# A two-level Winograd matmul: three more sums of A stored by the first column chunk, and a scheduler with uneven bandwidth shares

## Chip, cores and metric

One Trainium2 chip, one core of it. The metric is device time in microseconds (us): the median of several runs, here 1467.81 us before the change (three runs, 1466.79 to 1472.12).

## What is computed

`out = tanh(a @ b + bias)`, with `a` and `b` of 4096 x 4096 float32, `bias` of 4096 float32 added to each row, `out` float32. The kernel multiplies in fp16 with float32 sums in PSUM.

```python
def reference(a, b, bias):
    return np.tanh(np.matmul(a, b) + bias)
```

## The kernel before

**Tiling.** The output's 4096 columns are worked in four **chunks** of 1024 (`NCW`); the 4096 rows in 16 **pairs** of 2 x 128 rows, and two pairs (512 rows) make a **group**, in the code a `duo`, numbered 0 to 7. For one pair and one chunk the matmul is a 2 x 2 block matmul: A in four blocks a11, a12, a21, a22 of 128 rows x 2048, B in b11 to b22 of 2048 x 512. It is done with Strassen's seven products in Winograd's form (`work`, L885): P1 = a11 b11, P2 = a12 b21, P3 = s4 b22, P4 = a22 t4, P5 = s1 t1, P6 = s2 t2, P7 = s3 t3. The sums of A are s1 = a21 + a22, s2 = s1 - a11, s3 = a11 - a21 = a22 - s2, s4 = a12 - s2. A **plain** product is 16 matmuls of 128 x 128 by 128 x 512 per pair. A **fine** product does the same once more, with the two pairs of a group as the two block rows: seven smaller products (p1 to p7) of eight matmuls with 256 columns, 56 matmuls for the group in the place of 32 of double width. For a fine product the left operand is needed in three combinations of the two pairs, y, z and v (`fine_left`, L611), the right one as f1, f2, f3, f4 (`fine_right`, L749).

**Chunks.** The first chunk begins with eight 128-row blocks done as an ordinary matmul, while B arrives; then groups 2 to 7 run with Strassen at one level, and `STEEP[0]` gives how many of P1, P7, P5 are fine in each of the six groups: 0, 1, 1, 1, 1, 1. `natural` (L514) loads the four raw blocks of a pair through POOL's queue (`load_rows`, the cast to fp16 is in the DMA), transposes them on DVE, and makes the sums. The second to fourth chunk each go twice over the eight groups: `pass_one` (P1 and P2 of each group, and P6 in the last two chunks) in the order `ORDER[c]`, then `pass_two` (P7, P6, P5, P4, P3) in the reverse order.

**What is kept in HBM.** `scratch` (L409) has for each name and group a tensor with five slots of half a block: slots 1 and 2 hold the first pair p, 3 and 4 the second pair q with its halves swapped; slot 0 holds q.lo + q.hi - p.lo (`sigma`, L600). With slot 0 filled, a pass can fetch the group as a `Skew` (L569): y from slots 0 and 1, x from slots 2 and 3, without a sum on DVE. `keep` (L542) writes slots 1 to 4, `move` (L530) issues one DMA on SP's queue, 512 KB for two slots and 256 KB for one. In the first chunk groups 2 to 7 store a11, a12, a22 and s2 so. In the second chunk's second pass `lowers` (L1160) sends these groups to `all_skewed` (L1176): fetch a22, s2, a11, a12 as skews (s2 with half a block more, for its plain P6), make s3, s1 and s4 by `skew_sum`, two DVE operations of 128 x 2048 each, and store the three for the later chunks. Groups 0 and 1 aren't stored by the first chunk but for pair 0: the second chunk loads their raw blocks through POOL (`upper`, L1216, in the first pass; `others`, L1226, in the second, where the sums are made too).

**What sets the order.** Nothing is ordered by hand below that. Every operation is added to a `Plan` (L134) with an engine, an estimated duration, what it reads and writes, and for transfers the bytes. `rank` gives each a due time from its successors; `schedule` (L216) then lets five queues (PE, DVE, ACT, POOL, SP) run against each other in an event loop, takes buffers from 51 places of SBUF (`PLACES`) when an operation may start, and the order in which operations start there is the order in which they are emitted. PE keeps the order in which its work was added. On the chip each engine goes through its list in that fixed order and waits by semaphores: an operation that waits holds back all behind it. Transfers in the model share bandwidth: each has a rate and a latency (`DMA`), and `flow` (L275) gives every queue that has something under way the same share. `FARTHER` (L38) limits how far ahead of PE, in us of due time, a chunk's later loads of B (b12, b22) may be taken up.

Of the kernel before, what the change touches and what calls it, by code (L numbers as in the profile page):

```python
# [10 lines left out]
P = 128  # L11
# [6 lines left out]
TP = T // 2  # L18
# [5 lines left out]
ADD = mybir.AluOpType.add  # L24
SUB = mybir.AluOpType.subtract
# [5 lines left out]
KEPT = (("a11",), ("s1", "a22", "s4"), ("a11", "a12", "s3", "s2", "s1", "a22", "s4"), ())  # L31
NEAR = 12.0
REACH = 20.0
ORDER = ((2, 3, 4, 5, 6, 7), (7, 6, 0, 5, 1, 4, 3, 2), (2, 0, 1, 3, 4, 5, 6, 7), (7, 6, 5, 4, 3, 2, 1, 0))
SUMS = tuple(range(16))
SOFT = 1.5
BEHIND = 2
FARTHER = (50, 60, 50, 50)  # L38
THREE = (False, False, True, True)
LATER = 6  # L40
HOLD = (1, 1, 1, 1)
FIRST = (0,)
WHOLE = ()
SPARE = ("a11", "a12", "a22")
HELD = ("s1", "s3", "s4")
PLAIN = (0, 0, 0, 0)
SMALL = 5
RING = 8
DMA = {"POOL": (380e3, 3.75), "LATER": (380e3, 6.0), "in": (405e3, 3.1), "out": (315e3, 2.8)}
RISE = ((), (4, 4, 4, 4, 4, 4, 4, 4), (4, 4, 4, 4, 4, 4, 4, 4), (4, 4, 4, 4, 4, 4, 4, 4))  # L50
SECONDS = (0, 8, 8, 8)
STEEP = ((0, 1, 1, 1, 1, 1), (0, 1, 2, 2, 2, 2, 2, 2), (0, 3, 3, 3, 3, 3, 3, 3))
BASIS = ("a11", "a12", "a22", "s2")
STORED = BASIS + ("s1", "s3", "s4")
LEFT = ("P6", "P7", "P5", "P4", "P3")
# [78 lines left out]
class Plan:  # L134
# [81 lines left out]
    def schedule(self):  # L216
# [38 lines left out]
        def fits(op):  # L255
# [16 lines left out]
                    return False  # L272
            return not want or op.due <= at_pe[0] + min(op.reach, op.far if op.early else 1e9)

        def flow(now):  # L275

            live = [p for p in pipes.values() if p]
            for p in live:
                p[0][0] -= (now - clock[0]) / len(live)
            clock[0] = now  # L280
            ended = False
            for p in live:
                while p and p[0][0] < 1e-6:
                    op = p.pop(0)[1]
                    op.done = now + op.wait
                    heapq.heappush(events, (op.done, op.n, 1))
                    ended = True
            return ended

        def next_flow(now):  # L290
            live = [p for p in pipes.values() if p]
            if live:
                clock[1] += 1
                at = now + max(min(p[0][0] for p in live), 1e-6) * len(live)
                heapq.heappush(events, (at, clock[1], 3))

        while events:
# [74 lines left out]
def kernel(  # L372
# [62 lines left out]
    def tt(o, x, y, op, n, reads, writes, wide=True, **kw):  # L435
        dve(n, lambda: nc.vector.tensor_tensor(out=o(), in0=x(), in1=y(), op=op), reads, writes, wide, **kw)  # L436
# [4 lines left out]
    def at(buf, *key):  # L441
        key = key if len(key) > 1 else key[0] if key else slice(None)
        return lambda: buf[key]
# [86 lines left out]
    def move(name, duo, first, tl, t0, n, out, **kw):  # L530

        box = scratch[name, duo]
        dram_, key = (box, range(first, first + n)), (ALL, ds(t0 * TP, n * TP))
        sb = tl if out else (tl, range(t0, t0 + n))

        def emit():
            far, near = box[ALL, ds(first, n)], tl[key].rearrange("p (n t) m -> p n t m", n=n)
            nc.sync.dma_start(out=far if out else near, in_=near if out else far)

        add("SP", 0.34, emit, (sb if out else dram_,), (dram_ if out else sb,), nbytes=P * n * TP * P * 2, **kw)  # L540
# [56 lines left out]
            tt(at(o), at(u), at(v), op, T * P, (u, v), (o,), wide=False)  # L597
        return Skew(name, None, here)

    def sigma(name, duo, pq):  # L600

        p, q = (s[name] for s in pq)
        v = new("v" + name, [P, TP, P], cls="out")
        tt(at(v), at(q, ALL, ds(0, TP)), at(q, ALL, ds(TP, TP)), ADD, TP * P, (q,), (v,), wide=False, soft=6.0)
        tt(at(v), at(v), at(p, ALL, ds(0, TP)), SUB, TP * P, (v, (p, (0,))), (v,), wide=False, soft=6.0)
        move(name, duo, 0, v, 0, 1, True, soft=6.0)
        skewed.add((name, duo))

    skewed, held_names = set(), {}
# [275 lines left out]
    def work(duo, name, s, part=None, last=True):  # L885

        d, c, k, bop, pair = duo, duo.c, duo.k, duo.bop, duo.pairs[s]
        left, right, bank = {
            "P1": ("a11", "b11", D), "P2": ("a12", "b21", D), "P7": ("s3", "t3", I), "P6": ("s2", "t2", Z),
            "P5": ("s1", "t1", C), "P3": ("s4", "b22", C), "P4": ("a22", "t4", Z),  # L890
        }[name]
        bank = bank[s]
        a_ = d.a[s]
        if name == "P3" and "s4" not in a_:
            asum(a_, "s4", "a12", "s2", SUB, over=None if d.stays else "s2")
            if c == 1 and not d.parts and pair in SUMS:
                keep(pair, a_, ("s4",))
                whole.add(pair)
        t0, nt = (0, T) if part is None or name == "P3" else (part * TP, TP)
        start = name == "P1" or (name == "P7" and part != 1)  # L900
        product(bank, a_[left], [bop.get((right, i)) for i in range(4)], t0, nt, start)
        b1 = k["b1"]
        if name == "P1":
            after_p1(d, s, part)
        elif name == "P7":
            if part != 0:
                d.p7[s] = new("p7", [P, NB], fp32, "out")
                copy(at(d.p7[s]), at(bank), NB, (bank,), (d.p7[s],))
                after_p7(d, s, part)
        elif name == "P6":  # L910
            after_p6(d, s, part)
        elif name == "P5":
            if part == 0:
                return
            after_p5(d, s)
        elif name == "P2":
            if part == 0:
                e = d.aside[s] = [new("aside", [P, NB], fp32, "out" if i == 2 else "big") for i in range(0)]
                d.as11[s] = (d.box[s], 0)
                copy(at(d.box[s], ALL, 0), at(bank), NB, (bank,), ((d.box[s], (0,)),))  # L920
# [735 lines left out]
    for c in range(NC):  # L1656
        duos = [[2 * i, 2 * i + 1] for i in ORDER[c]]
        if c >= TWO:
            k = load_bias(c)
            finish_bias(k)  # L1660
            bop, rights = {}, {}
            for name in ("b11", "b21"):
                for blk in range(4):
                    raw_b(bop, c, name, blk, NEAR)
            rights["P1"] = fine_right(bop, "b11", True, NEAR)
            if SECONDS[c]:
                rights["P2"] = fine_right(bop, "b21", True, NEAR)
            if before:
                waiting.append(lambda between, before=before: (before(), between()))

            def rest():
                for blk in range(4):
                    for name in ("b12", "b22"):
                        raw_b(bop, c, name, blk, (NEAR, FARTHER[c]))
                    bsums(bop, blk, (NEAR, FARTHER[c]))

            if THREE[c]:
                rest()
                rights["P6"] = fine_right(bop, "t2", True, NEAR)
            on_chip = pass_one(c, k, bop, rights, duos, held)  # L1680
            if not THREE[c]:
                rest()
            pass_two(c, k, bop, rights, duos[::-1], on_chip)
            before = held = None
            continue
        fines = {}
        for i, pairs in enumerate(duos):
            d = Duo()
            d.c, d.k, d.bop, d.pairs = c, k, bop, sorted(pairs)
            d.parts = c > 0 and i == 0  # L1690
            d.last = d.stays = i == len(duos) - 1 and c < TWO - 1
            d.x = STEEP[c][i]
            duo = d.pairs[0] // 2
            d.a = [natural(p, p in early, i == 0, SPARE if p % 2 and duo not in WHOLE else ()) for p in d.pairs]
            for name in () if duo in WHOLE else BASIS if i == 0 else BASIS[1:]:
                sigma(name, duo, d.a)
            if d.x and not d.parts:
                for name, r in (("P1", "b11"), ("P7", "t3"), ("P5", "t1"))[:d.x]:
                    if name not in fines:
                        fines[name] = fine_right(bop, r)  # L1700
            d.right = fines
            before = run_duo(d, before)
            held = d.a
    def place_tile(buf):
# [44 lines left out]
```

## Time and profile before

| what | value |
|---|---|
| median of three runs | 1467.81 us |
| lowest, highest | 1466.79, 1472.12 us |
| the profiled execution's own time | 1469.58 us |
| its span, first to last instruction | 1467.9 us |
| DMA, mean over the span | 266 GB/s, 390.43 MB |
| POOL's queue (q0), the casting loads | 73.44 MB as written |
| SP's queue (q1) | 315.15 MB |
| second chunk's first pass, about | 405 to 520 us |
| second chunk's second pass, about | 520 to 770 us |

The profile has one execution with each instruction's start and end. PE is the tensor engine's matmuls, PEld its weight loads, DVE the vector engine, ACT the scalar engine, POOL and SP two engines that here issue transfers; a name with q (SPq, POOLq) is an engine's DMA issue. `b<-in_b_dram` reads: tile b, written from tensor in_b_dram. In names of tiles the numbers are left out, `parts` are small float32 or half-size buffers that share a place, `nat` are raw tiles of A. L436 and L439 are the helpers for all DVE sums and ACT copies, L771 and L786 the matmuls of plain and fine products; so the tiles tell them apart, not the line. In a group's line the time after the bar is its busy total, then the mean of one in ns, then the idle time of its engine just before it and what ended that.

### The profile page before, as it was taken

How to read it: one execution, taken by the hardware profiler on the slowest of the kernel's cores; microseconds unless marked ns; L12 is line 12 of the kernel's file. 1: busy time of each engine (PE TensorE's matmuls, PEld its weight loads, DVE VectorE, ACT ScalarE, POOL GpSimd, SP SyncE). 2: the span in 40 equal slices, each digit the busy share in tenths (PEclk: the TensorE clock that was granted, in tenths of full speed). 3: DMA queues.
4: the chain of work that ended last, by engine and by line, in shares of the span. 5: the costliest groups of instructions: out<-in, count | busy, mean ns of one | idle time of the engine just before them, and what ended most of it. 6: DMA issues, size and time to landing. Idle time of an engine off the chain costs nothing.

```text
span 1467.9 us, 28825 instructions
## 1 busy us (share of the span) xinstructions
PE 1445.8 (98%) x11232; PEld 1098.5 (75%) x11232; DVE 1116.6 (76%) x1716; ACT 459.6 (31%) x1056; POOL 303.7 (21%) x565
## 2 busy tenths in 40 slices
PE   9999999999999999899999999999999999999998
PEld 4444545555478877678878888888888888888887
DVE  3557877666857898888788799976778678986765
ACT  2111211121133424243343332334333333243433
POOL 8754433434333001010131300000111310000000
PEclk9999999999999999999999999999999999999999
DMA  9999999999999979999999988778999988678773
GB/s 177 190 234 259 270 244 227 262 237 228 264 273 298 333 238 327 286 345 334 336 314 322 294 267 290 234 259 272 255 286 339 244 238 292 231 246 271 262 256 110
DMA packets 196873, 390.43 MB, mean 266 GB/s; under 512 B 25728, under 2 KB 91776, under 8 KB 196736
## 3 DMA queue, kind: packets, MB, share of 16 engines
q1 hardware_dynamic: 114048, 315.15, 61.5%
q0 software_dynamic: 82688, 73.44, 32.1%
q8 instruction: 88, 1.44, 0.4%
q14 instruction: 49, 0.40, 0.1%
HBM read 320.86 MB, written 141.03 MB: 315 GB/s over the span
## 4 chain that ended last, share of the span: by engine, by line
PE 73%; DMA 16%; DVE 5%; POOL 3%; issue 2%; ACT 1%; DVEq 0%; POOLq 0%; ACTq 0%; SPq 0%
PE ps L786 54%; PE ps L771 18%; DMA b<-in_b_dram 8%; DMA nat<-in_a_dram 5%; DMA land<-in_a_dram 2%; POOL b L698 2%; POOL land L492 1%; DVE parts L436 1%; DMA st<-state 1%; DVE ps L436 0%; DMA out_dram<-parts 0%; DMA xs<-s 0%; DVE a L468 0%; DMA a<-a 0%; DVE b L436 0%
## 5 line engine op out<-in xcount | busy, mean ns | idle before, releaser
L698 POOL DMA_DIRECT2D b<-in_b_dram x256 | 137.6, 541 | 538.1 <-DVE ps L436 203.6
L439 ACT COPY ps<-ps 128x256 f32<-128x256 f32 (+1 forms) x289 | 106.0, 367 | 336.6 <-PE ps L786 322.4
L492 POOL DMA_DIRECT2D nat<-in_a_dram x240 | 129.1, 543 | 334.1 <-PE ps L786 165.9
L786 PEld LDWEIGHTS <-ya 128*128 128x128 f16 x1424 | 139.3, 98 | 17.4
L786 PEld LDWEIGHTS <-zs 128*128 128x128 f16 x1408 | 138.0, 98 | 19.0 <-DVE b L436 0.8
L786 PEld LDWEIGHTS <-xa 128*128 128x128 f16 x1152 | 112.9, 98 | 26.0 <-issue 11.4
L786 PEld LDWEIGHTS <-za 128*128 128x128 f16 x1232 | 120.6, 98 | 14.2 <-issue 0.2
L786 PEld LDWEIGHTS <-ys 128*128 128x128 f16 x1216 | 118.9, 98 | 16.1 <-DVE ys L436 2.3
L439 ACT COPY parts<-ps 128x256 f32<-128x256 f32 (+1 forms) x182 | 70.9, 390 | 163.4 <-DVE ps L436 74.8
L786 PEld LDWEIGHTS <-parts 128*128 128x128 f16 x1104 | 108.0, 98 | 12.7 <-DVE parts L436 0.3
L771 PEld LDWEIGHTS <-s 128*128 128x128 f16 x624 | 61.0, 98 | 74.7 <-DVE s L436 2.8
L436 DVE TENSOR_TENSOR parts<-ps,parts 128x256 f32<-128x256 f32 (+1 forms) x172 | 75.2, 437 | 52.8 <-PE ps L786 46.2
L771 PEld LDWEIGHTS <-a 128*128 128x128 f16 x624 | 61.0, 98 | 72.0 <-DVE a L436 1.0
L786 PEld LDWEIGHTS <-xs 128*128 128x128 f16 x1056 | 103.2, 98 | 15.0 <-issue 1.6
L1547 PE MATMUL ps<-b,o 128*128 128x512 f16 x512 | 111.4, 379 | 0.7 <-DVE ps L1572 0.6
L468 DVE STREAM_TRANSPOSE a<-nat 128x512 uint32<-128x512 uint32 x120 | 78.2, 688 | 38.3 <-PE ps L771 21.4
L436 DVE TENSOR_TENSOR ps<-ps,parts 128x256 f32<-128x256 f32 (+1 forms) x187 | 83.0, 445 | 28.6 <-PE ps L786 15.7
L786 PE MATMUL ps<-b,zs 128*128 128x256 f16 x768 | 100.2, 274 | 0.5 <-DVE b L436 0.5
L1547 PEld LDWEIGHTS <-o 128*128 128x128 f16 x512 | 49.8, 98 | 60.9 <-issue 1.2
L624 DVE TENSOR_TENSOR zs<-xs,ys 128x2048 f16<-128x2048 f16 x66 | 80.4, 1218 | 17.6 <-PE ps L786 16.1
L771 PE MATMUL ps<-t,s 128*128 128x512 f16 x400 | 88.0, 379 | 2.3 <-DVE s L436 2.3
L771 PE MATMUL ps<-b,a 128*128 128x512 f16 x384 | 85.0, 379 | 0.5 <-DVE a L436 0.5
(140 smaller groups left out, 2576.2 us busy)
## 6 DMA issues: line engine op xcount, KB each, us to landing
ya<-a SPq DMA_DIRECT2D x72, 512.0 KB, 6.3
xa<-a SPq DMA_DIRECT2D x72, 512.0 KB, 6.3
ys<-s SPq DMA_DIRECT2D x66, 512.0 KB, 5.1
xs<-s SPq DMA_DIRECT2D x66, 512.0 KB, 4.9
b<-in_b_dram POOLq DMA_DIRECT2D x256, 128.0 KB, 8.0
nat<-in_a_dram POOLq DMA_DIRECT2D x240, 128.0 KB, 7.0
out_dram<-parts SPq DMA_DIRECT2D x112, 256.0 KB, 6.2
a<-a SPq DMA_DIRECT2D x32, 512.0 KB, 6.3
```

Of the source, the lines that this page charges most:

```text
L436: dve(n, lambda: nc.vector.tensor_tensor(out=o(), in0=x(), in1=y(), op=op), reads, writes, wide, **kw)
L439: act(n, lambda: nc.scalar.copy(o(), x()), reads, writes, **kw)
L468: nc.vector.transpose(dst[ALL].rearrange("P t m -> P (t m)").bitcast(pair32).rearrange("P (U m) -> P U m", m=P)[:, ds(t0 // 2, nu), ds(row ...
L492: nc.gpsimd.dma_start(out=tl[(ds(q * QP, QP), *key)], in_=src)
L624: nc.vector.tensor_tensor(out=halves(z), in0=halves(x), in1=halves(y)[:, ds(0, 1)].broadcast_to([P, 2, TP * P]), op=SUB,)
L698: nc.gpsimd.dma_start(out=dst.rearrange("p t j n -> p t (j n)") if j is None else dst, in_=src)
L771: nc.tensor.matmul(bank[ALL], left_tile(left, k + t + shift), rb.tile(t), start=start and k == t0 and t == 0, stop=k + t == t0 + nt - 1, s ...
L786: nc.tensor.matmul(bank[ALL, HALF[half]], left_tile(buf, at_ * TP + i * TB + t), rb.tile(t), start=False, stop=i == 1 and t == TB - 1, ski ...
L1547: nc.tensor.matmul(bank[ALL], left_tile(left, t), rb.tile(tb), start=start, stop=stop, skip_group_check=True,)
```

## The change

Four things are changed. (1) Groups 2, 3, 4 and 5 also store s1, s3 and s4 in the first chunk, each with slot 0 (`AHEAD`, `put_by`), and are marked `whole`, so that the second chunk's second pass fetches s3, s2, s1, a22 and s4 and doesn't call `all_skewed` for them. Groups 6 and 7 stay as they were. (2) The second chunk's order has group 0 in fourth and group 1 in sixth place, where they were third and fifth; `STEEP[0]` ends with 2, so group 7's P7 is fine in the first chunk; `FARTHER` is 40 for the last two chunks. (3) The scheduler's rates and latencies are others, and `rates` replaces equal shares: when POOL's queue and SP's both have something under way, SP's has 0.64 if its first transfer is a load and 0.47 if it is a store, and POOL's has the rest. (4) `sigma` takes how soft its due time is.

```diff
-ORDER = ((2, 3, 4, 5, 6, 7), (7, 6, 0, 5, 1, 4, 3, 2), (2, 0, 1, 3, 4, 5, 6, 7), (7, 6, 5, 4, 3, 2, 1, 0))
+ORDER = ((2, 3, 4, 5, 6, 7), (7, 6, 5, 0, 4, 1, 3, 2), (2, 0, 1, 3, 4, 5, 6, 7), (7, 6, 5, 4, 3, 2, 1, 0))
-FARTHER = (50, 60, 50, 50)
+FARTHER = (50, 60, 40, 40)
+AHEAD = (("s1", "s3", "s4"), ("s1", "s3", "s4"), ("s1", "s3", "s4"), ("s1", "s3", "s4"), (), ())
-DMA = {"POOL": (380e3, 3.75), "LATER": (380e3, 6.0), "in": (405e3, 3.1), "out": (315e3, 2.8)}
+DMA = {"POOL": (384e3, 3.65), "LATER": (384e3, 5.0), "in": (399e3, 3.86), "out": (369e3, 3.5)}
+SHARE = (0.64, 0.47)
-STEEP = ((0, 1, 1, 1, 1, 1), (0, 1, 2, 2, 2, 2, 2, 2), (0, 3, 3, 3, 3, 3, 3, 3))
+STEEP = ((0, 1, 1, 1, 1, 2), (), ())
...
+        def rates():
+
+            live = [(e, p) for e, p in pipes.items() if p]
+            if len(live) == 1:
+                return [(live[0][1], 1.0)]
+            part = {p[0][1].eng: SHARE[p[0][1].soft is not None or not p[0][1].bufs] for _, p in live if p[0][1].hw}
+            return [(p, 1 - sum(part.values()) if e == "POOL" else part[e]) for e, p in live]
+
         def flow(now):
-
-            live = [p for p in pipes.values() if p]
-            for p in live:
-                p[0][0] -= (now - clock[0]) / len(live)
+            shares = rates() if any(pipes.values()) else []
+            for p, r in shares:
+                p[0][0] -= (now - clock[0]) * r
...
+    def put_by(d, name, s):
+
+        keep(d.pairs[s], d.a[s], (name,), spare=(name,) if s else ())
+
-    def sigma(name, duo, pq):
+    def sigma(name, duo, pq, soft=6.0):
...
         if name == "P3" and "s4" not in a_:
             asum(a_, "s4", "a12", "s2", SUB, over=None if d.stays else "s2")
-            if c == 1 and not d.parts and pair in SUMS:
-                keep(pair, a_, ("s4",))
-                whole.add(pair)
+            if "s4" in d.put:
+                put_by(d, "s4", s)
+                if s:
+                    sigma("s4", pair // 2, d.a, 12.0)
...
+            d.put = AHEAD[i]
+            for name in d.put:
+                if name != "s4":
+                    for s in range(2):
+                        put_by(d, name, s)
+                    sigma(name, duo, d.a, 12.0)
+            for p in d.pairs if d.put else ():
+                held_names[p] = set(d.put)
+                if d.put == HELD:
+                    whole.add(p)
             before = run_duo(d, before)
```

The branch `c == 1 and not d.parts` that goes was never taken, since only the first chunk comes there; so were the second and third entries of `STEEP`.

More of the change, by code (lines that the diff above doesn't have):

```diff
@@ L273, in fits @@
             return not want or op.due <= at_pe[0] + min(op.reach, op.far if op.early else 1e9)
+        def rates():
[4 more added lines that the diff above has]
+            return [(p, 1 - sum(part.values()) if e == "POOL" else part[e]) for e, p in live]
         def flow(now):
-            live = [p for p in pipes.values() if p]
-            for p in live:
-                p[0][0] -= (now - clock[0]) / len(live)
+            shares = rates() if any(pipes.values()) else []
+            for p, r in shares:
+                p[0][0] -= (now - clock[0]) * r
             clock[0] = now
             ended = False
-            for p in live:
+            for p, _ in shares:
                 while p and p[0][0] < 1e-6:
@@ L290, in next_flow @@
         def next_flow(now):
-            live = [p for p in pipes.values() if p]
-            if live:
+            if any(pipes.values()):
                 clock[1] += 1
-                at = now + max(min(p[0][0] for p in live), 1e-6) * len(live)
+                at = now + min(max(p[0][0], 1e-6) / r for p, r in rates())
                 heapq.heappush(events, (at, clock[1], 3))
@@ L598, in skew_sum @@
         return Skew(name, None, here)
-    def sigma(name, duo, pq):
+    def put_by(d, name, s):
+        keep(d.pairs[s], d.a[s], (name,), spare=(name,) if s else ())
+    def sigma(name, duo, pq, soft=6.0):
         p, q = (s[name] for s in pq)
         v = new("v" + name, [P, TP, P], cls="out")
-        tt(at(v), at(q, ALL, ds(0, TP)), at(q, ALL, ds(TP, TP)), ADD, TP * P, (q,), (v,), wide=False, soft=6.0)
-        tt(at(v), at(v), at(p, ALL, ds(0, TP)), SUB, TP * P, (v, (p, (0,))), (v,), wide=False, soft=6.0)
-        move(name, duo, 0, v, 0, 1, True, soft=6.0)
+        tt(at(v), at(q, ALL, ds(0, TP)), at(q, ALL, ds(TP, TP)), ADD, TP * P, (q,), (v,), wide=False, soft=soft)
+        tt(at(v), at(v), at(p, ALL, ds(0, TP)), SUB, TP * P, (v, (p, (0,))), (v,), wide=False, soft=soft)
+        move(name, duo, 0, v, 0, 1, True, soft=soft)
         skewed.add((name, duo))
```

## The prediction

> **What bounds the kernel now.** I read the busy table first, then the waits of the tensor engine (PE), then the stages in which they fall.
>
> ```profile
> PE   1445.8 (98%) x11232; PEld 1098.5 (75%) x11232; DVE 1116.6 (76%) x1716; ACT 459.6 (31%) x1056; POOL 303.7 (21%) x565
> PE 73%; DMA 16%; DVE 5%; POOL 3%; issue 2%; ACT 1%; DVEq 0%; POOLq 0%; ACTq 0%; SPq 0%
> ```
>
> PE is busy 1445.8 of 1467.9 us. Unless the change takes matmuls away, everything it can win is in the other 22.1 us. Where they are is told by the busy time in stages (columns: stage, its length, busy of PE, PEld, DVE, ACT, POOL, then granted clock, DMA share, GB/s):
>
> ```profile
> 0.00:142.00 142.00, 136.62 (x633) 61.25 (x634) 74.99 (x111) 26.73 (x49) 91.79 (x172) 1.00 1.15 213
> 142.00:405.00 263.00, 262.53 (x1354) 132.37 (x1355) 194.22 (x289) 49.80 (x93) 101.98 (x190) 1.00 1.04 247
> 405.00:460.00 55.00, 53.91 (x461) 44.91 (x460) 33.60 (x57) 19.57 (x46) 20.41 (x38) 1.00 1.06 278
> 460.00:550.00 90.00, 89.21 (x766) 74.54 (x765) 84.10 (x123) 29.21 (x71) 7.66 (x15) 1.00 0.92 292
> 595.00:620.00 25.00, 21.13 (x168) 16.71 (x166) 23.18 (x34) 4.78 (x12) 1.61 (x3) 0.93 0.89 276
> 760.00:840.00 80.00, 76.61 (x697) 67.93 (x696) 63.43 (x105) 28.53 (x68) 22.17 (x42) 1.00 1.09 311
> 1080.00:1135.00 55.00, 51.73 (x467) 45.47 (x466) 46.05 (x77) 19.37 (x46) 6.45 (x12) 1.00 0.97 318
> 1205.00:1468.00 263.00, 259.19 (x2373) 231.90 (x2371) 201.02 (x324) 93.01 (x229) 0.00 (x0) 1.00 0.71 236
> ```
>
> The start lacks 5.4 us, the end 3.8; the change leaves the code of both alone. Between them: the first chunk's groups 0.5; the second chunk's first pass (405 to 550) 1.1 + 0.8; its second pass at 595 to 620 3.9, and 7% of clock over 25 us is 1.7 more, 5.6 together; the turn to the third chunk 3.4; the turn to the fourth 3.3. Every stage that isn't listed is full but for 0.1. So some 14 us are within reach, and the largest piece is at 600. Its chain:
>
> ```profile
> 588.95 11.62 DMA nat<-in_a_dram
> 600.69 0.10 DVE a L468
> 602.23 1.21 DVE L436 TENSOR_TENSOR s<-a,a 128x2048 f16<-128x2048 f16 x1
> 608.54 1.23 DVE L436 TENSOR_TENSOR a<-a,a 128x2048 f16<-128x2048 f16 x1
> PE ps L786 <- DVE ys L436: 2.0, 1, 2.0
> PE ps L786 <- DVE ps L436: 1.8, 2, 1.5
> 612.00:615.60 3.60, 3.28 (x17) 2.14 (x16) 3.50 (x7) 1.68 (x4) 0.00 (x0) 0.53 0.02 7
> ```
>
> Group 1, whose rows of A come raw, has its last raw tile landing near 600.6; behind it stand DVE's transposes, sums and quarters in a fixed order, and PE waits 2.0 us for the quarter sum `ys`, 1.8 for PSUM work queued behind the sums. Then PE runs 3.6 us at a clock of 0.53, which costs 1.7. The Trainium skill (TensorE: Matmul & The Clock Gate, Part 1) states that the clock halves after an idle window of some 3.4 us and returns after as long a busy one; the return agrees with the 3.6 us, the fall here came after less idle time than that.
>
> **The change, part by part.** *The sums.* All six groups 2 to 7 now rebuild s1, s3 and s4 in the second chunk, with six 128x2048 operations each; in the built order of the changed kernel 24 of those 36 are gone:
>
> ```profile
> L436 DVE TENSOR_TENSOR ys<-ya,ys 128x2048 f16<-128x2048 f16 x6 | 7.3, 1219 | 0.2 <-DMA out_dram<-p 0.2
> L436 DVE TENSOR_TENSOR xa<-xa,xs 128x2048 f16<-128x2048 f16 x6 | 7.3, 1213 | 1.0 <-DMA xa<-a 1.0
> L436 DVE TENSOR_TENSOR parts<-parts,s 128x1024 f16<-128x1024 f16 x6 | 4.1, 681 | 0.1
> L436 DVE TENSOR_TENSOR ps<-ps,parts 128x256 f32<-128x256 f32 x175 | 74.8, 428 | 28.6 <-PE ps L786 15.7 <-ACT parts L439 8.1
> ```
>
> DVE loses 24 x 1.22 = 29.2 us in the second pass and gains 4 groups x 3 names x 2 x 0.68 = 16.3 us in the first chunk. None of this is PE time. Its worth is that PSUM work (0.43 us each) stands behind such sums: 460 to 550 has DVE busy 84.1 of 90, and the groups before 600 are 7.3 us of DVE work lighter each. In the first chunk a group lasts 47.5 us:
>
> ```profile
> 237.50:285.00 47.50, 47.50 (x249) 24.25 (x248) 32.81 (x46) 9.23 (x17) 18.97 (x37) 1.00 1.06 248
> ```
>
> DVE has 32.8 of 47.5 in use there; 4.1 more hide under PE. Without that cover they would cost up to 16.3.
>
> *The transfers.* Each name costs 512 + 256 + 256 KB of stores on SP's queue per group: 3.15 MB (decimal), 12.6 MB in all, in the first chunk. In the second pass a group's loads grow from 4.25 to 5 MiB and 3 MiB of stores go: 2.25 MiB less. What room has the first chunk? Its four groups from 142 to 332 us, and the fullest 50 us of the trace:
>
> ```profile
> q0 software_dynamic: 19948, 18.17, 62.6%
> q1 hardware_dynamic: 13318, 28.72, 40.9%
> ...
> q1 hardware_dynamic: 3877, 11.49, 62.8%
> q0 software_dynamic: 4297, 3.91, 47.7%
> ...
> q1 hardware_dynamic: 114048, 315.15, 61.5%
> 560.00:568.00 8.00, 8.00 (x74) 6.97 (x72) 7.51 (x10) 2.76 (x8) 0.00 (x0) 1.00 1.04 412
> ```
>
> q0 casts from f32 to f16, so its source is twice what is counted. From 142 to 332 us the first pair moves 2 x 18.17 + 28.72 = 65.1 MB, 343 GB/s. POOL ran ahead in that stretch; what a group itself needs is 8 raw tiles of 1.05 MB and 28.72 / 4 = 7.2 MB beside them, 15.6 MB, and with the change 18.7 in 47.5 us, 394 GB/s. The second pair (450 to 500) moved 386, and hardware transfers alone reach 412. So the added stores take all the room that is left: at 386 GB/s four groups fall behind by 8 x 190 = 1.5 MB, one and a half tiles, and two groups without the stores follow, in which it drains. The stores themselves have no due time; on SP's queue they wait for their sums, and behind them stand only other stores until the second chunk's first loads, two groups later. I take +0.5 us, between nothing and what the rival below costs, near nothing since 386 is the nearest row. The Trainium skill (DMA: Bandwidth & Descriptors, Specifications) gives about 358 GB/s as a core's share of HBM, which speaks against the change; the 412 and 386 above are over it, so I don't take it for a ceiling here, but it is a rival.
>
> *One more fine product.* Group 7's P7 goes from 32 matmuls of 512 columns to 56 of 256:
>
> ```profile
> 227.70 37.99 PE ps L771 x176
> 629.00 18.34 PE ps L786 x168
> ```
>
> That is 32 x 0.2159 = 6.9 us against 56 x 0.1092 = 6.1: 0.8 us less of PE, the only matmul time that changes. Its eight new 128x1024 sums of B and four of A (12 x 0.68 = 8.2 us of DVE) fall into a group with 14.7 us of DVE to spare; if that cover were gone, they would eat the 0.8 and up to 7 more.
>
> *Order and scheduler.* Bandwidth shares, latencies, the new order of groups and the farther limit of 40 act only through the static order. I counted in both built orders, for each raw load on POOL, its room: the PE work between the instruction that frees its buffer and the matmul that is late if the load's first DVE reader, or something queued behind that reader, is late. A block of 1.05 MB is four issues; what they take shows here:
>
> ```profile
> 741.88 2.16 POOL L698 DMA_DIRECT2D b<-in_b_dram  x4 [29.68 <-DMA out_dram<-st]
> 587.30 0.54 POOL L492 DMA_DIRECT2D nat<-in_a_dram  x1 [1.13 <-DMA nat<-in_a_dram]
> 588.95 0.54 POOL L492 DMA_DIRECT2D nat<-in_a_dram  x1 [1.11 <-DMA nat<-in_a_dram]
> nat<-in_a_dram POOLq DMA_DIRECT2D x16, 128.0 KB, 10.2
> b<-in_b_dram POOLq DMA_DIRECT2D x24, 128.0 KB, 11.1
> b<-in_b_dram POOLq DMA_DIRECT2D x12, 128.0 KB, 13.3
> ```
>
> 2.2 us if POOL is free, else 1.65 apart, some 5; then 10.2 us (at 578 to 600), 11.1 (450 to 500) or 13.3 (1095 to 1130) to landing. So a load wants 12 to 18 us of room. Before, the raw tiles of the second chunk's first pass have 10.1, 13.9 and 15.9, group 1's lower tiles at 600 14.5 to 19.9, the last blocks of b22 there 15.1 and 14.5: too little, and just where PE waits. After: 18.1 and more, 17.1 to 20.3, 15.9 and 18.5. At the turn to the fourth chunk b21's least room goes from 18.7 to 23.1. At the turn to the third, b11 stays at 16.5 and 16.3. On the other side, with the limit of 40 the b22 blocks of the third and fourth chunk have as little as 12.8, where the least of b12 and b22 was 15.9.
>
> *The sum.* 405 to 550: 1.9 to 0.3, -1.6. Around 600: 5.6 to 0.6, -5.0 (POOL room up by some 2.5 us, a lighter DVE before it; once the wait is short, the slow clock goes with it; what is late next is the second pair's `ys`, 0.6). Turn to the third chunk -0.3, to the fourth -2.3. P7 -0.8. First chunk +0.5. Late b22 +0.8, between nothing and 4 us each. Together -8.7. The profiled execution took 1469.58 us (span 1467.9 and 1.7 around it) and would take 1460.9; it stood 1.8 above the median of 1467.81, so I forecast 1459.1 for the median.
>
> **Rivals.** *The waits move.* b22 with 12.8 us of room against up to 18: two of them late by 4 us are 8 us. For it speaks the room, against it that the loads' neighbours have 16 or more. It gives 1467: within 0.5% of no change (7.3 us, about what a measurement can tell). *The first chunk becomes a matter of DMA: slower.* If the 343 GB/s of 142 to 332, at a share of 1.04, are already what this mix of small raw packets and stores can do, a group of 18.7 MB takes 54.5 us, 7.0 too long; four lack 28, and the time is 1486.6. It decides where the backlog outgrows the buffers: of 51, B holds 28, so some ten tiles late in stores (10 MB, a ceiling of 394 - 53 = 341) stop the raw tiles for certain, and a few late ones already do where DVE queues behind them. For it: the share over 1 and buffers that late stores hold. Against: 386 in another mix, and that only 0.5 of 263 us are lost there now. By the skill's 358 GB/s the group would take 52.2 us, and four groups would give about 1477. *More goes.* If the fitted shares also end the waits at both turns (3.1 + 1.0), with no late b22 (0.8) and a free first chunk (0.5), 5.4 more go: 1453.7. That the sums are still built in the second chunk isn't open: the built order lacks them.
>
> **How the numbers follow.** Forecast 0.45 (1455 to 1464), more goes 0.18, waits move 0.24, DMA 0.13. Faster by over 0.5% means below 1460.5: all of "more goes", about three quarters of the forecast, a little of the moved waits: 0.55. Slower by over 0.5%, above 1475.1: 0.14, nearly all DMA. Within: 0.31. Range 1450 to 1471: it leaves out the DMA case and a few hundredths below.
>
> **What would show it.** In the changed profile: 24 of the 36 rebuilt sums gone; around group 1's raw tiles (some 32 us earlier) PE waits under 1 us and the clock is 1.00; PE full in the first chunk at about 390 GB/s of source and store; b21's waits at the fourth chunk's turn halved. I am wrong if PE lacks over 3 us between 142 and 405, or if DVE waits over 3 us for b in the second half of a chunk's first pass.

## The result, and the profile after

The changed kernel takes 1463.85 us (median of six runs, 1462.51 to 1466.24), beside 1468.65 for the kernel before on the same chip (six runs, 1466.79 to 1472.12): a ratio of 0.9965 [0.9950, 0.9980], or -0.35%. That is clear of the noise, but by the prediction's bound of 0.5% it is no change. The time lies in the range, 4.8 us above the forecast of 1459.1; the likeliest class ("faster by over 0.5%", 0.55) did not come. The range of 1450 to 1471 held "no change" as well, so lying in it says little; the stages below say more. The profiled execution took 1466.24 us with a span of 1464.5, 3.4 less than before. It is the slowest of the six, 2.4 above their median, so the stages account for a gain of 3.4 us where the medians differ by 4.8.

The busy table and the chain of the page:

```profile
PE 1444.2 (99%) x11256; PEld 1101.4 (75%) x11256; DVE 1112.8 (76%) x1739; ACT 461.3 (31%) x1062; POOL 304.3 (21%) x565
PE 74%; DMA 11%; DVE 3%; issue 1%; POOL 1%; ACT 0%; SPq 0%; DVEq 0%; POOLq 0%
```

PE stands 20.3 us instead of 22.1. The stages of the prediction (busy of PE, PEld, DVE, ACT, POOL, then clock, DMA share, GB/s), with the first chunk and the stretch around 600 cut finer:

```profile
0.00:142.00 142.00, 139.65 (x646) 62.84 (x647) 78.81 (x117) 26.99 (x50) 90.90 (x170) 1.00 1.16 225
142.00:160.00 18.00, 13.55 (x51) 5.45 (x50) 16.65 (x31) 1.22 (x2) 8.41 (x16) 0.81 1.16 282
160.00:405.00 245.00, 244.93 (x1302) 127.26 (x1300) 187.43 (x287) 49.36 (x95) 90.66 (x168) 1.00 1.08 277
405.00:460.00 55.00, 54.95 (x459) 44.69 (x457) 38.86 (x65) 18.41 (x44) 19.47 (x36) 1.00 1.13 307
460.00:550.00 90.00, 87.46 (x768) 74.93 (x766) 81.29 (x126) 34.01 (x80) 16.52 (x31) 1.00 0.94 275
550.00:620.00 70.00, 70.00 (x566) 55.02 (x564) 54.01 (x83) 25.88 (x59) 9.37 (x18) 1.00 0.98 307
620.00:640.00 20.00, 19.00 (x157) 15.04 (x155) 13.28 (x19) 4.74 (x13) 0.00 (x0) 1.00 0.74 237
760.00:840.00 80.00, 76.75 (x700) 68.21 (x698) 61.74 (x103) 29.32 (x69) 17.55 (x33) 1.00 1.07 315
1080.00:1135.00 55.00, 54.63 (x501) 48.84 (x500) 50.72 (x84) 20.92 (x50) 4.29 (x8) 1.00 0.97 326
1135.00:1230.00 95.00, 93.51 (x854) 83.37 (x853) 69.94 (x106) 34.80 (x84) 17.25 (x32) 1.00 0.89 250
```

The stretch around 600 is full now, at a clock of 1.00: that piece was won. The turn to the fourth chunk (1080 to 1135) lacks 0.4 instead of 3.3. The turn to the third (760 to 840) is as before. The second chunk's first pass gained nothing by this count: 405 to 460 lacks 0.1 instead of 1.1, 460 to 550 lacks 2.5 instead of 0.8. New is the second row: in 18 us PE is busy 13.55, at a clock of 0.81, where the row of before (142 to 405) lacked 0.5 in all.

Busy time hides part of a loss, since a late or slowed matmul counts as busy. So for the table below I took the start of every matmul from each trace: a stage's loss is its length, less 0.2159 us for each matmul of 512 columns and 0.1092 for each of 256 that starts in it. "Tail" is the time after the last matmul. Every ratio is to runs of the kernel before on the same chip.

| kernel | ratio to before [95%] | 110-160 | 160-405 | 405-520 | 520-650 | 760-850 | 1080-1230 | tail |
|---|---|---|---|---|---|---|---|---|
| before | 1 | 2.7 | 0.5 | 2.1 | 7.5 | 4.2 | 4.6 | 3.8 |
| after | 0.9965 [0.9950, 0.9980] | 7.3 | 0.2 | 3.0 | 1.6 | 3.9 | 2.4 | 4.9 |
| e1 scheduler alone | 1.0024 [1.0007, 1.0041] | 4.6 | 0.0 | 1.6 | 10.9 | 5.5 | 2.7 | 3.8 |
| e2 sums alone | 1.0084 [1.0069, 1.0099] | 1.9 | 3.0 | 18.7 | 1.8 | 5.9 | 0.2 | 4.1 |
| e3 group 2 not stored | 1.0000 [0.9988, 1.0012] | 5.1 | 0.1 | 4.4 | 7.4 | 3.6 | 0.2 | 3.9 |
| e4 no sums stored | 1.0027 [1.0014, 1.0039] | 5.4 | 0.0 | 4.4 | 14.5 | 2.8 | 1.4 | 3.8 |
| e5 limit 50 | 0.9969 [0.9952, 0.9985] | 7.6 | 1.2 | 2.8 | 0.1 | 2.8 | 2.7 | 4.1 |
| e6 six groups stored | 1.0062 [1.0042, 1.0083] | 4.9 | 0.6 | 18.4 | 0.5 | 0.9 | 0.9 | 4.3 |
| e8 old order | 0.9975 [0.9959, 0.9991] | 6.9 | 0.4 | 1.1 | 0.1 | 3.7 | 4.8 | 4.3 |
| e9 old scheduler | 1.0091 [1.0060, 1.0123] | 0.7 | 7.9 | 11.8 | 1.9 | 4.5 | 5.1 | 4.3 |
| e10 old scheduler at the start | 0.9984 [0.9972, 0.9996] | 2.9 | 5.8 | 2.4 | 1.7 | 3.6 | 1.6 | 4.1 |
| e11 e10, three groups | **0.9942 [0.9921, 0.9963]** | 1.8 | 0.0 | 4.9 | 1.3 | 2.0 | 0.7 | 3.9 |
| e12 e10, plain P7 | 0.9970 [0.9954, 0.9985] | 1.8 | 0.9 | 4.9 | 1.7 | 2.9 | 0.8 | 4.1 |
| e13 e11, old order | 0.9941 [0.9921, 0.9961] | 2.9 | 0.0 | 5.5 | 0.4 | 5.9 | 1.4 | 3.9 |

From before to after: -5.9 at 520 to 650, -2.2 at 1080 to 1230 (-3.7 until 1140, +1.5 behind), -0.3 at 760 to 850, -0.8 of matmul time; against these +4.6 at 110 to 160, +0.9 at 405 to 520, +1.1 in the tail; the rest is -0.7. Together -3.3, and the span is 3.4 shorter. A stage's figure is from one execution, and runs of one kernel lie up to 11 us apart, so differences of 1 or 2 us between rows are not read, and the sums of such terms below account for these two executions, not for the kernels. e13's row is from the slowest of its five runs, 3.7 us above their median.

**Where the new loss sits.** PE of the changed kernel around 142, then its waits at 142 to 405:

```profile
136.78 5.99 PE L783 MATMUL ps<-t,s 128*128 128x512 f16 x27
147.22 9.76 PE L783 MATMUL ps<-t,s 128*128 128x512 f16 x32 [4.45 <-DVE ps L444]
```

```profile
PE ps L783 <- DVE ps L444: 4.5, 1, 4.5
```

PE stands 4.45 us for one PSUM addition, and the next 32 matmuls take 9.76 us where 32 x 0.2159 is 6.9. It is the only wait of PE in the first chunk's groups. DVE's list in that time, in the changed kernel and then in the kernel before:

```profile
142.16 0.69 DVE L444 TENSOR_TENSOR parts<-parts,s 128x1024 f16<-128x1024 f16 x1
142.76 1.29 DVE L444 TENSOR_TENSOR t<-b,t 128x1024 f16<-128x1024 f16 x2
143.97 0.69 DVE L444 TENSOR_TENSOR parts<-parts,s 128x1024 f16<-128x1024 f16 x1
145.87 0.71 DVE L476 STREAM_TRANSPOSE a<-nat 128x512 uint32<-128x512 uint32 x1 [1.21 <-DMA nat<-in_a_dram]
146.50 0.67 DVE L444 TENSOR_TENSOR ps<-ps,bias 128x512 f32<-128x512 f32 x1
```

```profile
143.59 1.30 DVE L468 STREAM_TRANSPOSE a<-nat 128x512 uint32<-128x512 uint32 x2
144.81 0.67 DVE L436 TENSOR_TENSOR ps<-ps,bias 128x512 f32<-128x512 f32 x1
145.39 0.67 DVE L436 TENSOR_TENSOR parts<-parts,s 128x1024 f16<-128x1024 f16 x1
```

The addition `ps<-ps,bias` that frees PE stands behind sums for slot 0 (`parts`), sums of B and a transpose whose raw tile has not landed: 1.21 us of DVE's delay is that tile, the rest is work that could have come later. In the kernel before, a sum of the same kind stands behind the addition.

### The profile page after: what moved, and what is told of

It reads as the page before. It is cut to its first block, busy times and chain, and to the rows that moved or that the text cites. A ratio compares the mean times of both kernels' runs of the same rounds, so it can differ in the third digit from the quotient of the medians.

```text
span 1464.5 us, 28902 instructions
## 1 busy us (share of the span) xinstructions
PE 1444.2 (99%) x11256; PEld 1101.4 (75%) x11256; DVE 1112.8 (76%) x1739; ACT 461.3 (31%) x1062; POOL 304.3 (21%) x565
## 4 chain that ended last, share of the span: by engine, by line
PE 74%; DMA 11%; DVE 3%; issue 1%; POOL 1%; ACT 0%; SPq 0%; DVEq 0%; POOLq 0%
PE ps L798 57%; PE ps L783 18%; DMA b<-in_b_dram 6%; DMA nat<-in_a_dram 3%; DMA a<-a 1%; DVE parts L444 1%; DMA bias<-in_bias_dram 0%; DMA out_dram<-parts 0%; DVE ps L444 0%; DVE zs L636 0%; POOL nat L500 0%; DMA out_dram<-p 0%; DMA ys<-s 0%; DVE a L476 0%; DVE s L444 0%
## 5 line engine op out<-in xcount | busy, mean ns | idle before, releaser
L798 PEld LDWEIGHTS <-ys 128*128 128x128 f16 x1360 | 133.1, 98 | 15.4
L783 PEld LDWEIGHTS <-s 128*128 128x128 f16 x752 | 74.2, 99 | 90.2 <-issue 8.9
L798 PEld LDWEIGHTS <-ya 128*128 128x128 f16 x1296 | 126.8, 98 | 16.0
L798 PEld LDWEIGHTS <-xs 128*128 128x128 f16 x1184 | 115.8, 98 | 17.8 <-issue 2.2
L783 PE MATMUL ps<-t,s 128*128 128x512 f16 x528 | 121.1, 385 | 4.5 <-DVE ps L444 4.5
L798 PEld LDWEIGHTS <-xa 128*128 128x128 f16 x1024 | 100.2, 98 | 14.6 <-issue 2.7
L783 PEld LDWEIGHTS <-a 128*128 128x128 f16 x592 | 57.9, 98 | 67.7
L636 DVE TENSOR_TENSOR zs<-xs,ys 128x2048 f16<-128x2048 f16 x74 | 90.1, 1218 | 15.4 <-PE ps L798 11.5
L636 DVE TENSOR_TENSOR za<-xa,ya 128x2048 f16<-128x2048 f16 x60 | 73.1, 1218 | 17.0 <-DMA out_dram<-cs 10.5
```

The source lines that it names most:

```text
L636: nc.vector.tensor_tensor(out=halves(z), in0=halves(x), in1=halves(y)[:, ds(0, 1)].broadcast_to([P, 2, TP * P]), op=SUB,)
L783: nc.tensor.matmul(bank[ALL], left_tile(left, k + t + shift), rb.tile(t), start=start and k == t0 and t == 0, stop=k + t == t0 + nt - 1, s ...
L798: nc.tensor.matmul(bank[ALL, HALF[half]], left_tile(buf, at_ * TP + i * TB + t), rb.tile(t), start=False, stop=i == 1 and t == TB - 1, ski ...
```

## The experiments

My first theory: the new sums of group 2 (`parts` in the list above; of the two `parts<-parts,s`, one stands in e4's list too, which stores none of them) displaced the addition. The rival: the scheduler's new rates and shares, which reach the start too though no code there changed, put filler work ahead of it.

**e1, the scheduler alone**, and **e2, the sums alone.** Both are made from the changed kernel; in both, `ORDER`, `FARTHER` and `STEEP` are those of before.

```diff
 # e1
+AHEAD = ((), (), (), (), (), ())
...
 # e2
+DMA = {"POOL": (380e3, 3.75), "LATER": (380e3, 6.0), "in": (405e3, 3.1), "out": (315e3, 2.8)}
-            part = {p[0][1].eng: SHARE[p[0][1].soft is not None or not p[0][1].bufs] for _, p in live if p[0][1].hw}
-            return [(p, 1 - sum(part.values()) if e == "POOL" else part[e]) for e, p in live]
+            return [(p, 1 / len(live)) for _, p in live]
```

> The new scheduler (rates, latencies, uneven shares) alone: nothing stored ahead, the old order of groups, the old farther limits, P7 of group 7 plain. Theory 1 (the 7.5 us that PE loses at 142 to 153 us come from the sums that group 2 adds on DVE there): the start of the first chunk's groups loses 3 to 4 us as in the kernel before; the first pass of the second chunk and the turn to the fourth chunk gain about 3 us by more room for POOL's loads; group 1's place near 600 us still loses 2 or more, since DVE keeps its 29 us of sums; in all 1465 to 1467. Theory 2 (that loss comes from the scheduler's new order of loads and sums at the start): PE loses 7 us there without any sums too, 1469 to 1471.

> Only the sums of groups 2 to 5 stored by the first chunk; the old rates and equal shares, old order of groups, old farther limits, P7 of group 7 plain. Theory 1: PE loses 5 us or more at 142 to 153 us here too; 595 to 620 us gains 3 to 5; 760 to 840 and 1080 to 1135 lose 3.4 and 3.3 as before; in all 1466 to 1469. Theory 2: the start loses 3 to 4 as before, in all 1463 to 1465.

Measured: 1474.11 us (ratio 1.0024) and 1481.34 (1.0084). Both are slower than either theory had them. Each part alone makes the kernel slower, by 0.2% and 0.8%; the whole change wins 0.35%. The scheduler alone keeps the loss around 600 (10.9) and has the new loss at 142 (4.6); the sums alone end the first and don't have the second (1.9), but lose 18.7 at 405 to 520. In e2 the waits of PE there, and the loads in the chain behind them:

```profile
PE ps L797 <- DVE ps L443: 10.2, 5, 3.3
```

```profile
483.66 15.13 DMA b<-in_b_dram
...
499.07 12.98 DMA b<-in_b_dram
```

Blocks of B that land 13 to 15 us after issue hold DVE, 4.6 us from 440 to 520, raw tiles of A another 5.7, and PSUM work stands behind.

**e3, group 2 not stored, and e4, no sums at all**, both with the new scheduler and order.

```diff
 # e3
+AHEAD = ((), ("s1", "s3", "s4"), ("s1", "s3", "s4"), ("s1", "s3", "s4"), (), ())
 # e4
+AHEAD = ((), (), (), (), (), ())
```

> The changed kernel, but group 2, the first that the first chunk works with Strassen, stores no sums ahead (groups 3, 4 and 5 do). Theory 1: PE loses at most 3.5 us at 139 to 160 us and the clock stays 1.00 there; group 2 costs 7.3 us of DVE in the second pass again, hidden; 1459 to 1461. Theory 2: 7 us are still lost at the start, 1463 to 1465.

> The changed kernel with nothing stored ahead: new scheduler, new order of groups, limit of 40, fine P7, but all six groups build their sums in the second chunk. If the sums' removal was worth what I put on it (a lighter DVE before group 1's raw tiles), 550 to 640 us loses 3 to 5 us and 460 to 550 another 1, while the start of the first chunk loses 3 to 4 in place of 7.5: 1463 to 1466, so about the changed kernel's time. If the gain was the scheduler's and the order's alone, nothing is lost in the second chunk and the start is cheaper: 1459 to 1461.

Measured: 1468.95 us (1.0000) and 1473.37 (1.0027). The stages 110 to 160 and 520 to 650 of e3, then of e4:

```profile
110.00:160.00 50.00, 46.77 (x210) 20.77 (x208) 43.90 (x72) 6.62 (x12) 23.35 (x44) 0.97 1.14 267
520.00:650.00 130.00, 125.64 (x1008) 99.12 (x1006) 107.97 (x164) 43.92 (x102) 12.87 (x24) 0.99 0.86 268
```

```profile
110.00:160.00 50.00, 46.35 (x209) 20.42 (x207) 43.02 (x71) 6.62 (x12) 22.07 (x41) 0.97 1.15 264
520.00:650.00 130.00, 119.09 (x944) 92.30 (x942) 112.81 (x164) 40.72 (x95) 12.92 (x24) 0.97 0.88 286
```

Both times lie above the ranges of either theory, so the theories are judged by the stages alone. Two things follow. First, my theory on the start falls for the most part: with no sum of group 2 the stage still lacks 3.2 and 3.7 us and some clock (5.1 and 5.4 in the table, 7.3 with the sums; e6, which has the sums of group 2 too, loses 4.9). Second, the sums stored ahead are what ended the wait around 600: 14.5, 7.4 and 1.6 us are lost there with none, three and four groups stored, everything else alike. It isn't the number of groups that counts: e11 below stores three as well, but leaves out group 5 in place of group 2, and loses 1.3. The second pass goes through the groups in the reverse order, so that group 2 stands just ahead of groups 3 and 1, and group 5 behind them. Storing them takes operations from DVE and 2.25 MiB of transfers per group from the second pass; which of the two does it was not tried.

**e9, the old rates and equal shares everywhere, and e10, only at the start.** The rest is the changed kernel's. e10 uses the old rates for what is added up to the first Strassen group, and equal shares until 150 us of the model's time.

```diff
 # e9
+DMA = {"POOL": (380e3, 3.75), "LATER": (380e3, 6.0), "in": (405e3, 3.1), "out": (315e3, 2.8)}
...
+            return [(p, 1 / len(live)) for _, p in live]
 # e10
+START = {"POOL": (380e3, 3.75), "LATER": (380e3, 6.0), "in": (405e3, 3.1), "out": (315e3, 2.8)}
+UNTIL = 150.0
+            rate = START if self.young else DMA
...
+            if clock[0] < UNTIL:
+                return [(p, 1 / len(live)) for _, p in live]
```

> The changed kernel with the old rates, latencies and equal shares; order, limits, sums and fine P7 as in the change. If the old shares are what the sums-only kernel lost by, 10 or more are lost at 440 to 520 us: 1470 or more. If it was the old order of groups, 440 to 520 loses under 4, and the start, with the old shares, 2 to 3: 1459 to 1463.

> The changed kernel, but the scheduler uses the old rates and equal shares for all that is added up to the first Strassen group and until 150 us of its own clock; sums stored ahead as in the change. In DVE's list the PSUM addition on which PE waited at 142 us then stands ahead of the two last half-size sums and of four products of sums for B. Theory A (PE lost 7.3 us there because the new rates expect transfers late and put filler work ahead of that addition): 2 to 3 us lost at 110 to 160 us and no slow clock, 4 to 5 less in all: 1459 to 1460. Theory B (raw tiles come late because the stores ahead take bandwidth): 6 or more still lost there, 1463 to 1465.

Measured: 1481.48 us (1.0091) and 1465.91 (0.9984). e10's stages 110 to 160 and 160 to 405 and the four us behind its longest wait, then that wait, then e9's stages 160 to 405 and 440 to 520:

```profile
110.00:160.00 50.00, 47.55 (x220) 21.14 (x218) 42.33 (x66) 6.90 (x13) 22.20 (x41) 1.00 1.15 283
160.00:405.00 245.00, 241.19 (x1276) 125.30 (x1274) 188.18 (x288) 47.79 (x93) 88.73 (x165) 0.99 1.08 278
374.00:378.00 4.00, 4.00 (x24) 2.95 (x22) 3.08 (x5) 0.36 (x1) 1.32 (x3) 0.57 1.12 170
```

```profile
PE ps L804 <- DVE a L450: 3.0, 1, 3.0
```

```profile
160.00:405.00 245.00, 239.60 (x1265) 124.04 (x1264) 184.41 (x284) 47.06 (x92) 85.80 (x159) 0.99 1.06 273
440.00:520.00 80.00, 71.65 (x629) 62.45 (x628) 67.31 (x103) 25.96 (x62) 22.99 (x43) 0.96 1.11 305
```

The rival holds: with the old estimates at the start alone, and all the sums kept, the wait for the addition is gone (2.9 lost, as before the change). But the time doesn't follow. What was won at 142 is lost near 374, where a sum of A is late for a fine product. The changed kernel, which stopped at 142, loses 0.2 in that stage; that its stop gave the later work time is argued, not shown. Counted from 110 to 405, before loses 3.2, the changed kernel 7.5 and e10 8.7: with four stored groups and a fine P7 in group 7, the first chunk pays some 4 to 6 us in one place or the other (e12 below, with the four groups and a plain P7, loses 2.7). e9 shows the worth of rates and shares in the second chunk: 11.8 us lost at 405 to 520, against 3.0, with the same order of groups; it is 1.26% slower than the changed kernel (1.0091 to 0.9965). Which of the two, rates or shares, does it was not tried.

**e11, group 5 not stored; e12, group 7's P7 plain; e6, all six stored.** e11 and e12 start from e10, e6 from the changed kernel.

```diff
 # e11
+AHEAD = (("s1", "s3", "s4"), ("s1", "s3", "s4"), ("s1", "s3", "s4"), (), (), ())
 # e12
+STEEP = ((0, 1, 1, 1, 1, 1), (), ())
 # e6
+AHEAD = (("s1", "s3", "s4"),) * 6
```

> The run with the old rates at the start (PE lost 2.9 us at 110 to 160 us but 5.8 at 200 to 405, with a slow clock at 374) but group 5 stores no sums ahead: 3.15 MB less on SP's queue at 285 to 345 us, where group 7's raw tiles come in. Theory A (those raw tiles are late because the stores ahead share the DMA engines with them): 200 to 405 loses under 1.5 us, no slow clock there; group 5's sums come back in the second pass, far from group 1, and cost 0 to 2: 1460 to 1463. Theory B (PE waits there for DVE, which has group 7's quarter sums of t3 for the fine P7 in front): 200 to 405 still loses 4 or more, 1464 to 1467.

> The run with the old rates at the start and group 7's P7 plain (0.8 us more of matmuls, eight sums of 128x1024 and four of the left operand less on DVE). Theory A (late raw tiles): 200 to 405 still loses 4 or more; 1465 to 1468. Theory B (DVE's sums for the fine P7 in front): under 1.5 us lost there, no slow clock; 1461 to 1463.

> The changed kernel with all six groups storing their sums ahead: 6.3 MB more of stores from 330 to 430 us, 15 us less DVE work at the end of the second chunk's second pass. Theory A (the first chunk's transfers have no room left): PE loses 3 us or more at 200 to 440 us that it doesn't lose now, nothing comes back in the second pass, where groups 6 and 7 stand last and DVE has time; 1466 to 1470. Theory B (there is room): 200 to 440 loses under 1, 1462 to 1465.

Measured: e11 1460.24 us (0.9942), e12 1464.23 (0.9970), e6 1478.08 (1.0062). e11's stage 160 to 405, then e12's:

```profile
160.00:405.00 245.00, 245.00 (x1303) 127.23 (x1302) 187.82 (x287) 49.03 (x94) 91.73 (x171) 1.00 1.07 272
```

```profile
160.00:405.00 245.00, 244.22 (x1271) 124.05 (x1270) 180.28 (x265) 46.89 (x88) 89.42 (x167) 1.00 1.09 283
```

In e6, PE at 405 to 440 and DVE's waits at 418 to 438:

```profile
405.00:440.00 35.00, 25.25 (x174) 17.66 (x173) 20.25 (x36) 7.68 (x19) 13.31 (x25) 0.89 1.13 298
```

```profile
DVE f2b L444 <- DMA b<-in_b_dram: 4.8, 2, 2.7
DVE a L476 <- DMA nat<-in_a_dram: 4.4, 1, 4.4
```

With six groups' sums the stores run on into the second chunk (one is issued at 416.6 us) and its first loads come late: 4.8 us of waiting for blocks of B, 4.4 for a raw tile, and PE lacks 9.75 of 35 us. That is like the prediction's DMA rival, two groups further on than it put it. But at 405 to 440 the transfers run as fast as in the changed kernel (298 and 301 GB/s) and blocks of B land no later after their issue (a median of 9.5 us, 11.5 there). The loads start late, the first raw tile's at 415.5 us instead of 411.1; that the stores ahead are what delays them is argued, not shown. With three groups nothing is lost at 160 to 405. What POOL's queue moves between 285 and 345 us, in e10 and then in e11 (packets, MB, share), speaks for a part of the transfers in it:

```profile
q0 software_dynamic: 5676, 5.18, 56.4%
```

```profile
q0 software_dynamic: 7453, 6.78, 69.2%
```

Without group 5's stores the casting loads move 1.6 MB more (3.2 MB at the source) in the same 60 us. But e11 also takes 6 x 0.68 = 4.1 us of sums from DVE, and e12, with nearly the transfers of e10 (5.38 MB on this queue), relieves DVE alone by 8.2 us of sums and loses 0.9 there. Either relief is enough to end the wait at 374; how it divides between transfers and DVE stays open. e11 is 0.58% faster than before and only e13 comes as low; against the changed kernel's 0.9965 [0.9950, 0.9980] its interval [0.9921, 0.9963] overlaps, so that lead is likely, not sure. Set on the median that the forecast was made for, 0.9942 x 1467.81 is 1459.3.

**e5, the farther limit at 50; e8, the old order of groups; e13, the old order on e11.**

```diff
 # e5
+FARTHER = (50, 60, 50, 50)
 # e8 and e13
+ORDER[1] = (7, 6, 0, 5, 1, 4, 3, 2)
```

> The changed kernel with the farther limit of 50 in the last two chunks, as before. If the limit of 40 makes the b22 blocks late, the 1.9 us that PE lacks at 1140 to 1230 us go to under 0.6, while 1080 to 1135 stays near 0.5: 1462. If the place of the waits in a late chunk is only how one static order happens to fall, the sum of 760 to 850 and 1080 to 1230 moves by 2 us or more either way.

> The changed kernel with the old order of groups in the second chunk (raw group 0 third, group 1 fifth). If the old order is what the sums-only kernel lost 17.7 us by at 440 to 520 us, 10 or more are lost there again: 1473 or more. If the old equal shares did that, 440 to 520 loses 2 to 5 us: 1464 to 1467.

> The run without group 5's sums (1460.24 us) with the old order of groups in the second chunk. If the new order is what puts raw tiles and b22 close together at 440 to 520 us (3.3 us lost there; 0.9 in the changed kernel with the old order, 2.8 with the new one), 440 to 520 loses about 1 and the whole is 1457 to 1459. If each edit only deals the waits anew, that stage may gain but the sum of all stages moves by 2 us or more the other way: 1461 to 1465.

Measured: 1464.87 us (0.9969), 1465.50 (0.9975), 1461.41 (0.9941). Neither setting has an effect that can be told from none: the intervals of e5 and e8 hold the changed kernel's 0.9965, and e13's ratio is that of e11 (0.9942). e8 has 1.1 lost at 405 to 520 with the old order, which had seemed a cure for that stage; on e11 the same order has 5.5 there, so it carried nothing over. I take it that each static order deals the waits of the later chunks anew; with one trace of each kernel that is not shown.

## Why the prediction was off, point by point

- **Around 600, -5.0: right; it is -4.2.** From 560 to 650 the loss fell from 5.8 to 1.6; 1.0 of what is left is in the row of 620 to 640. The rebuilt sums are gone as read from the built order, 24 of 36; two groups are left:

```profile
L444 DVE TENSOR_TENSOR xa<-xa,xs 128x2048 f16<-128x2048 f16 x2 | 2.4, 1223 | 1.4 <-DMA xa<-a 1.4
L444 DVE TENSOR_TENSOR ys<-ya,ys 128x2048 f16<-128x2048 f16 x2 | 2.4, 1220 | 0.6 <-PE ps L798 0.6
```

  The clock is 1.00 at the new place of group 1. But the prediction gave the order and POOL's room the first credit, and the lighter DVE the second; e4, with the new order and rates and no sums, loses 14.5 at 520 to 650, twice what the kernel before loses, and e8, with the old order and the sums, 0.1. It was the sums, those of group 2 above all.
- **First chunk, +0.5: the step that failed; it is +4.3** (110 to 405: 3.2 before, 7.5 after). Two steps of the prediction are wrong. "The change leaves the code of both alone" is true of the code, and the start's order moved all the same, for it comes from the same estimates: with the old ones at the start the 4.5 us wait for the addition is gone and the stage loses 2.9 (e10), with the new ones and no added sum it loses 5.4 (e4). And the cover for the added sums was read from a late group with 32.8 of 47.5 us in use, while the first Strassen group has hardly any: DVE was busy 42.22 of 50 at 110 to 160 before, and is busy 43.50 now. What the added sums cost there is at most the 2 us between e3 or e4 and the changed kernel, too little to be read.

```profile
110.00:160.00 50.00, 45.55 (x199) 19.97 (x198) 43.50 (x68) 6.02 (x11) 21.15 (x39) 0.93 1.15 288
```

  The prediction's own test, "I am wrong if PE lacks over 3 us between 142 and 405", was met: 4.5 us of standing, and the slow clock beside it (2.3 us of standing lay just ahead of 142 before). Its other test was not: in the second halves of the first passes DVE waits at most 1.1 us for b.
- **Transfers of the first chunk: the sum right, the consequence half right.** From 152 to 342 us the queues of the changed kernel moved:

```profile
q0 software_dynamic: 18268, 16.64, 54.0%
...
q1 hardware_dynamic: 16479, 36.81, 54.0%
```

  2 x 16.64 + 36.81 = 70.1 MB in 190 us, 369 GB/s (343 before, "about 390" foretold), and PE lost 0.2 at 160 to 405. By the Trainium skill (DMA: Bandwidth & Descriptors, Specifications) a core's share is some 358 GB/s. The 369 are over it, so the 1477 that this share gave did not come, nor did the rival's 1486.6. But e9 and e10 lose 7.9 and 5.8 us at 160 to 405, and in e6 PE lacks 9.75 just behind, so little slack is left; since e12 ends e10's loss without taking a transfer away, it isn't slack in the transfers alone.
- **405 to 550, -1.6:** at 405 to 560 the loss went from 3.8 to 3.0, -0.8. By busy time, as the prediction read the stage, 405 to 550 lacks 2.6 instead of 1.9, so no gain can be read here. The raw tiles had the room that was counted, and took more than the 10.2 us quoted: one for which DVE stood until 478 landed 12.8 us after issue, behind blocks of B with 13 to 14. The chain there:

```profile
437.13 14.10 DMA b<-in_b_dram
451.52 13.17 DMA b<-in_b_dram
464.97 12.79 DMA nat<-in_a_dram
```

- **The turns:** -0.3 at the third chunk as foretold; -3.7 at the fourth (until 1140) instead of -2.3. **Late b22:** +1.5 (1140 to 1230) instead of +0.8; e5 shows that the limit of 40 isn't worth a measurable time either way. **P7:** 1436.4 us of matmuls became 1435.6, -0.8 as foretold (24 matmuls more, by the counts and the two durations).
- **The tail**, +1.1, was not foretold. Its code didn't change, and over all the kernels it is 3.8 to 4.9 us; its cause stays open.

So the gain around 600 came, and by the cause that the prediction had put second; the term most in error is the first chunk's, put at +0.5. Of the 5.4 us between -8.7 and -3.3, the first chunk, the mis-sized term, is 3.8; the tail 1.1, late b22 0.7, 405 to 560 and 560 to 650 0.8 each; the fourth turn gave 1.4 back, and stages that weren't counted 0.4. e11, which relieves the first chunk, gives the forecast time, in part by luck: it loses 4.9 at 405 to 520, where the prediction left 0.3, and 2.0 and 0.7 at the two turns, where it left 3.9 and 3.1.

## What to carry to other kernels

Where a static scheduler sets the order, a change of its estimates is a change everywhere: compare the built order of each stage, unedited ones first, before a stage is costed at nothing. Read the cover for added work from the tightest group that gets it, not from a typical one. And test the parts of a joint change apart: here each half alone was slower than before (1.0024 and 1.0084), the whole faster, and the best versions (e11, e13) had less of one half and left the start out of the other.

## What the runs showed of the hardware

The clock fell after short waits. One wait of 3.0 us in e10 brought a clock of 0.57 over the four us behind it, and one of 2.8 us in e1 was enough as well. How much follows isn't set by the length of the wait. Ahead of the same 32 matmuls e1 stands 2.79 us, the changed kernel (its line is above) 4.45 and e5 5.07; the matmuls then take 8.75, 9.76 and 8.69 us. The 32 before them in the changed kernel took 7.07 at full clock, so the slow clock costs 1.7, 2.7 and 1.6. The lines of e1, of e5, and of those 32:

```profile
145.96 8.75 PE L783 MATMUL ps<-t,s 128*128 128x512 f16 x32 [2.79 <-DVE ps L444]
```

```profile
148.91 8.69 PE L783 MATMUL ps<-t,s 128*128 128x512 f16 x32 [5.07 <-DVE ps L444]
```

```profile
135.71 7.07 PE L783 MATMUL ps<-t,s 128*128 128x512 f16 x32
```

The Trainium skill (TensorE: Matmul & The Clock Gate, Part 1) has the halving after an idle window of about 3.4 us and calls the window free-running. That the cost varies agrees with such a window; that 2.8 us of standing was enough here does not agree with the 3.4. The 7.2 us that wait and slow clock make together in the changed kernel are nearly the whole loss of that stage (7.3).

Casting loads through POOL's queue take longer to land in the changed kernel's first chunk: the median raw tile lands after 8.7 us instead of 6.7, while the DMA share at 160 to 405 is 1.08 instead of 1.04. The rows of before (147 to 337 us) and of the changed kernel (152 to 342):

```profile
nat<-in_a_dram POOLq DMA_DIRECT2D x140, 128.0 KB, 6.7
```

```profile
nat<-in_a_dram POOLq DMA_DIRECT2D x126, 128.0 KB, 8.7
```

The stores aren't enough to explain it. With the same stores and the old scheduler (e2), and with the new scheduler and no stores (e4), the same rows (152 to 342) are near those of before; only both together lengthen the landing. Why is open.

```profile
nat<-in_a_dram POOLq DMA_DIRECT2D x125, 128.0 KB, 6.9
```

```profile
nat<-in_a_dram POOLq DMA_DIRECT2D x136, 128.0 KB, 7.0
```
